# Layout of the streamed weights and the x loads, order of the first products, operands moved to PSUM, and places of four small chains in a two-layer trunk

## The chip, the cores and the metric

The kernel runs on one core of one Trainium2 chip. The metric is the device time of one execution, in microseconds (us), as the median of three runs. PE is the matrix engine (TensorE), DVE the vector engine, ACT the scalar engine, POOL the engine for general work (GpSimd), and SP the engine whose queue issues the weight loads. SBUF is the on-chip memory of all engines; PSUM holds what PE accumulates, and DVE and ACT can read and write it too.

## The reference

Two layers over a sequence of S = 256 positions with D = 1024 channels, in float32. Cut to what matters:

```python
for l in range(2):
    h = rmsnorm(x, norm_mix[l]); p = h @ w_in[l] + b_in[l]      # 6144 columns: xm, z, a, g, g1, g2
    y_m = mlstm_branch(p[xm], p[z], ...)                         # conv, q/k/v by blocks of 4, 4 heads, @ w_down
    y_c = silu(layernorm(dwconv31(p[a] * sigmoid(p[g])))) @ w_pw + b_pw
    x = x + (sigmoid(p[g1]) * y_m + sigmoid(p[g2]) * y_c) @ w_out[l]
    x = x + cross_attention(rmsnorm(x), rmsnorm(mem), wq, wk, wv, wo)
    x = x + conv_ffn(rmsnorm(x), w_up, dwconv3, w_down)          # 2816 hidden channels, gated
return rmsnorm(x, final_norm)
```

The mLSTM heads weigh their scores by exp(-max(m - u, mask)), a 256 x 256 matrix per head that is zero above the diagonal, and then multiply them with v.

## The kernel before

Activations lie with channels on the 128 partitions and the 256 positions along the row. A float32 operand is split into a high and a low part, and a product is the sum of three matmuls, high by high, high by low and low by high (`three`, lines 94 to 96), or of two instructions (`two`, lines 89 and 90) where a high part is multiplied with both parts of the other at once.

The weights are streamed. A chunk is 256 columns by 1024 rows, 1 MB; SP's queue loads it into one of three `raw` tiles (line 154, the first chunk in two loads of 128 columns, line 152). Each half of 128 columns is split into one of five `wsp` tiles: ACT casts the high part (line 173; line 171 in two pieces for the first half), and the low part, raw less high part, is taken by POOL (line 177, two instructions) or DVE (line 179, one) by the table `ON_POOL`, which lists for each kind of chunk the numbers of those that POOL takes. PE then makes 24 matmuls of 128x256 with each half. The chunks come in a fixed order: `xm` (0 to 3), `g` and `a`, `k`, `v`, `z`, `g1`, `g2`, `mdown`, `pw`, `out`, then attention (`q`, `wo`), then the network (`ug`, `uv`, `dn`). The tile framework reorders the instructions by priority within what the data allow; a helper that is told to act after a given product is called a hook, (j, k) being half j after product k.

The names that matter here:

- `u` is x times the norm's weights, split into parts (lines 262 and 263). The norm's factor is applied after the products, as a row: `stats` sums squares over channels by a matmul with a column of means (line 306), DVE adds epsilon (308), POOL takes the power -0.5 (310), and `to_row` turns the result into a row by a matmul with the identity (298). Layer 0 sums its squares on DVE first (lines 915, 916) into `ssum`; later `Stream.add` adds a square per channel block to `ssum` (341 or 339, then 342).
- `gate_weights` (lines 372 to 392) folds the gate's weights into the block-diagonal ones, and POOL builds block-diagonal tiles of them, `bb` (line 427). Line 491 is PE's first use.
- `head` (569 to 587): PE spreads a row of maxima over the partitions (`pm`, named `sm` in the trace), DVE makes the exponent (573, 575), ACT the exponential (577), and DVE multiplies by the scores `sc` (579; the tile `sc` is a part of `ws`), giving the weights `wt` of the head's matmuls (584, 587).
- Line 458 is the long row of taps of the 31-wide convolution, on DVE, with its sum `cv` in PSUM and its input `u` in SBUF.
- `swish` takes the row of the layer norm (310, 298) and applies it (711).

Of the kernel before, what the change touches and what calls it, by code (L numbers as in the profile page):

```python
# [15 lines left out]
P = 128  # L16
# [18 lines left out]
ON_POOL = {"xm": (2, 3), "g": (0, 1, 2, 3), "a": (0, 1, 2, 3), "k": (0, 1, 2, 3), "v": (0, 1),  # L35
           "z": (0, 2, 3), "g1": (0, 1, 2, 3), "g2": (0, 1), "wo": (0, 1, 2),
           "uv": tuple(range(11))}
# [16 lines left out]
def trunk(ctx, tc, xT, memT, pvec, wgr, w_in, ml_w_down, cv_w_pw, w_out, xa_wq, xa_wk, xa_wv, xa_wo,  # L54
# [53 lines left out]
    def cols(w, c0, k0=0, k1=KT):  # L108
        return w[c0 // 256, :, k0:k1, :]
# [35 lines left out]
    def emit_loads(upto):  # L145
        while st["dma"] < min(upto, len(chunks)):
# [3 lines left out]
            if i == 0:  # L150
                for sl in (slice(0, P), slice(P, 2 * P)):
                    nc.sync.dma_start(raws[i][:, :, sl], ap[:, :, sl])
            else:
                nc.sync.dma_start(raws[i], ap)
            st["dma"] += 1

    def emit_splits(upto):

        while st["split"] < min(upto, 2 * len(chunks)):
            i, j = divmod(st["split"], 2)  # L160
            emit_loads(i + 1)
            if chunks[i][0][0] == "v":
                r = raws[i][:, 2 * j:2 * j + 2, :]
            else:
                r = raws[i][:, :, j * P:(j + 1) * P]
            both = wsp.tile([P, 2] + list(r.shape[1:]), F32R, tag="wsp", name=nm("wsp"))
            hi, lo = both[:, 0], both[:, 1]
            if st["split"] == 0:
# [27 lines left out]
    with tc.high_priority():  # L196
        nc.scalar.dma_start(pvs[0][:, 0:KT], pvec[0][:, 0:KT])
        emit_loads(1)
        for c2 in range(4):
            loaded = nc.scalar.dma_start(xs[:, 2 * c2:2 * c2 + 2, :], xT[:, 2 * c2:2 * c2 + 2, :])  # L200
# [68 lines left out]

    def proj(key, x2, hooks=None, halves=False, bank=None):  # L270
# [3 lines left out]
        for j, w in weights(key):  # L274
            ps = (bank or acc)([P, 2, S] if halves else [P, S])
            if st["use"] == 1:

                for n, (a, b) in enumerate(((0, 0), (0, 1), (1, 0))):
                    for k in range(KT):
                        nc.tensor.matmul(ps, w[:, a, k, :], x2[:, k, b], start=(n + k == 0), stop=(n == 2 and k == KT - 1))  # L280
                yield j, ps
                continue
# [19 lines left out]
    def inv_rms(q, eps, free=True, rv=None):  # L302

        pt = pcv.tile([P, S], F32, tag="cv", name=nm("cm")) if free else sm([P, S])
        for t in range(2):
            nc.tensor.matmul(pt[:, t:t + 1], q[:, t * P:(t + 1) * P], mean1[:, 0:1], start=True, stop=True)
# [6 lines left out]
    class Stream:  # L313
# [17 lines left out]
        def add(self, c, ps):  # L331
# [4 lines left out]
            else:  # L336
                q = scr.tile([P, S], F32, tag="t2", name=nm("sq"))
                if c == KT - 1:
                    nc.vector.tensor_tensor(q, xs[:, c, :], xs[:, c, :], op=ALU.mult)
                else:  # L340
                    nc.scalar.activation(q, xs[:, c, :], AF.Square)
# [30 lines left out]
    def gate_weights(l):  # L372
# [17 lines left out]
        gs = sml.tile([P, 3, 8, 8], F32, tag="gs", bufs=1, name=nm("gs"))  # L390
        for w in range(3):
            nc.vector.tensor_reduce(gs[:, w], wg[:, w].rearrange("p c d g -> p c g d"), axis=AX.X, op=ALU.add)
        return pws, mq, gs

    def mix(l, x):
        gates = None if l else gate_weights(l)
        xc, hs = planes("xch")
        at, ready, norms = int(l == 0), [], list(range(4))
        hooks = {(0, 4): x.stats, (1, 1): x.to_row} if at else x.hooks()
        for i in range(4):  # L400
            for j, ps in proj(("xm", l, i), x.u, hooks if i == at else None,
                              bank=sm if i == 1 and at else None):
# [33 lines left out]
        pws, mq, gs = gates or gate_weights(l)  # L436
        build(mq, bqk)
        nc.vector.tensor_copy(bv[:, :, P:P + 8], gs[:, 2])
# [130 lines left out]
        def head(h):  # L569
            pm = sm([P, S])  # L570
            nc.tensor.matmul(pm, pick[:, h:h + 1].broadcast_to([36, P]), mrow, start=True, stop=True)
            wt = scr.tile([P, 384], F32, tag="t2", name=nm("wt"))
            nc.vector.scalar_tensor_tensor(wt[:, 0:256], pm, ucol[:, 0, h:h + 1], later,
                                           op0=ALU.subtract, op1=ALU.max)
            nc.vector.scalar_tensor_tensor(wt[:, 256:384], pm[:, P:S], ucol[:, 1, h:h + 1],
# [434 lines left out]
```

## Time and profile before

| | before |
|---|---|
| runs | 1103.79, 1099.6, 1101.84 us; median 1101.84 |
| profiled execution | 1103.6 us, of which the span from the first to the last instruction is 1101.9 |
| PE, PEld | busy 1075.8 us (98%), 1009.8 us (92%) |
| DVE, ACT, POOL | 857.4 us (78%), 694.1 us (63%), 438.6 us (40%) |
| mean granted clock of PE | 0.986 of full speed |
| DMA | 185.39 MB, 168 GB/s; the weights' queue 45.6% of 16 engines |

A row of a timeline is a start, a busy time, engine, line, operation, output<-inputs and a count, with the idle time of the engine ahead of it and what ended that in brackets. The clock is given as a share of full speed: 1.00 is the level of 2.4 GHz, about 0.51 that of 1.2 GHz.

### The profile page before, as it was taken

What the parts mean: (1) busy time and instruction counts of PE and PEld (TensorE: products, weight loads), DVE (VectorE), ACT (ScalarE), POOL (GpSimd) and SP (SyncE); (2) the same over time, 40 slices, a digit from 0 to 9 for tenths busy, and PEclk for the clock granted to TensorE, in tenths of its full rate; (3) what the DMA queues carried; (4) which work ended last, traced back from release to release, by engine and by line L of the source; (5) the groups of instructions that cost most, each with busy time, mean ns of one, the idle gap of its engine ahead of it and who ended that gap; (6) DMA issues with size and microseconds to landing.
All of it is one profiled execution on the core that took longest, in us unless ns stands there. A gap on an engine that the chain in (4) does not pass through costs nothing.

```text
span 1101.9 us, 19628 instructions
## 1 busy us (share of the span) xinstructions
PE 1075.8 (98%) x7642; PEld 1009.8 (92%) x7642; DVE 857.4 (78%) x1701; ACT 694.1 (63%) x1132; POOL 438.6 (40%) x351
## 2 busy tenths in 40 slices
PE   7999799999999999999999999999999999999996
PEld 7999689999999998888899998999999999888885
DVE  5788898978866887776668998998787578877753
ACT  5887365556555678774458766565545558877641
POOL 3858448610023445330048584782000434544000
PEclk8999899999999999999999999999999999999998
DMA  6535335445443445555545263545454244554541
GB/s 225 226 116 175 131 116 205 178 153 207 177 156 112 159 179 199 191 181 186 207 154 214 86 208 135 191 159 195 183 188 166 107 153 145 205 211 170 190 152 39
DMA packets 28957, 185.39 MB, mean 168 GB/s; under 512 B 3136, under 2 KB 5184, under 8 KB 7744
## 3 DMA queue, kind: packets, MB, share of 16 engines
q1 hardware_dynamic: 27280, 179.32, 45.6%
q10 hardware_dynamic: 1584, 4.82, 1.3%
q8 instruction: 60, 0.98, 0.4%
q14 instruction: 33, 0.27, 0.1%
HBM read 183.08 MB, written 1.05 MB: 167 GB/s over the span
## 4 chain that ended last, share of the span: by engine, by line
PE 92%; DVE 3%; ACT 1%; DMA 1%; POOL 1%; issue 1%; ACTq 0%; DVEq 0%
PE acc L89 20%; PE acc L95 18%; PE acc L94 18%; PE acc L96 18%; PE acc L90 10%; PE sm L94 2%; PE sm L95 1%; PE sm L96 1%; DVE wt L579 1%; ACT wsp L173 1%; PE sm L512 1%; DMA xs<-in_xT_dram 1%; DVE u L263 1%; PE sm L501 1%; PE sm L491 1%
## 5 line engine op out<-in xcount | busy, mean ns | idle before, releaser
L177 POOL TENSOR_TENSOR wsp<-raw,wsp 128x512 fp32r<-128x512 f32 x312 | 405.5, 1331 | 367.2 <-ACT wsp L173 361.7
L173 ACT CAST wsp<-raw 128x1024 fp32r<-128x1024 f32 (+1 forms) x343 | 353.6, 1036 | 193.0 <-PE acc L96 103.8
L179 DVE TENSOR_TENSOR wsp<-raw,wsp 128x1024 fp32r<-128x1024 f32 (+1 forms) x188 | 230.7, 1228 | 79.6 <-ACT wsp L173 77.4
L89 PE MATMUL acc<-x,wsp 128*128 128x512 f32 x576 | 203.6, 399 | 0.0
L458 DVE SCALAR_TENSOR_TENSOR cv<-u,pv,cv 128x256 f32<-128x256 f32 x464 | 193.4, 479 | 3.1 <-ACT cv L451 3.1
L94 PE MATMUL acc<-x,wsp 128*128 128x256 f32 x640 | 183.3, 287 | 0.0
L95 PE MATMUL acc<-x,wsp 128*128 128x256 f32 x640 | 181.6, 284 | 0.0
L96 PE MATMUL acc<-x,wsp 128*128 128x256 f32 x640 | 181.2, 283 | 0.0
L90 PE MATMUL acc<-x,wsp 128*128 128x256 f32 x576 | 161.8, 281 | 0.0
L89 PEld LDWEIGHTS acc<-x,wsp 128*128 128x128 f32 x576 | 108.2, 188 | 26.9
L89 PE MATMUL acc<-hh,wsp 128*128 128x512 f32 x352 | 124.5, 399 | 0.0
L95 PEld LDWEIGHTS acc<-x,wsp 128*128 128x128 f32 x640 | 122.7, 192 | 0.3
L94 PEld LDWEIGHTS acc<-x,wsp 128*128 128x128 f32 x640 | 122.6, 192 | 0.4 <-issue 0.2
L96 PEld LDWEIGHTS acc<-x,wsp 128*128 128x128 f32 x640 | 122.7, 192 | 0.2 <-issue 0.2
L90 PEld LDWEIGHTS acc<-x,wsp 128*128 128x128 f32 x576 | 108.8, 189 | 0.0
L310 POOL TENSOR_TENSOR rv<-rv,mhalf 128x2 f32<-128x2 f32 x9 | 7.2, 804 | 248.1 <-DVE rv L308 248.1
L95 PE MATMUL acc<-u,wsp 128*128 128x256 f32 x360 | 102.6, 286 | 0.7 <-DVE u L263 0.7
L94 PE MATMUL acc<-u,wsp 128*128 128x256 f32 x360 | 103.0, 289 | 0.0
L96 PE MATMUL acc<-u,wsp 128*128 128x256 f32 x360 | 102.5, 286 | 0.0
L855 DVE SCALAR_TENSOR_TENSOR fy<-u,pv,fy 128x256 f32<-128x256 f32 x176 | 84.1, 483 | 19.9 <-ACT fy L852 18.3
L90 PE MATMUL acc<-hh,wsp 128*128 128x256 f32 x352 | 98.9, 281 | 0.0
L89 PEld LDWEIGHTS acc<-hh,wsp 128*128 128x128 f32 x352 | 66.1, 188 | 16.4
(263 smaller groups left out, 2419.4 us busy)
## 6 DMA issues: line engine op xcount, KB each, us to landing
raw<-in_w_in_dram SPq DMA_DIRECT2D x47, 1024.0 KB, 4.8
raw<-in_ffn_w_up_dram SPq DMA_DIRECT2D x44, 1024.0 KB, 4.8
raw<-in_ffn_w_down_dram SPq DMA_DIRECT2D x16, 1024.0 KB, 4.8
raw<-in_xa_wk_dram SPq DMA_DIRECT2D x8, 1024.0 KB, 4.7
raw<-in_xa_wv_dram SPq DMA_DIRECT2D x8, 1024.0 KB, 5.1
raw<-in_ml_w_down_dram SPq DMA_DIRECT2D x8, 1024.0 KB, 4.7
raw<-in_cv_w_pw_dram SPq DMA_DIRECT2D x8, 1024.0 KB, 4.8
raw<-in_w_out_dram SPq DMA_DIRECT2D x8, 1024.0 KB, 4.7
```

The source lines that it names most:

```text
L89: nc.tensor.matmul(ps, a[:, 0], b, start=first, stop=False)
L90: return nc.tensor.matmul(ps[:, 1], a[:, 1], b[:, 0], start=False, stop=last)
L94: nc.tensor.matmul(ps, a[:, 0], b[:, 0], start=first, stop=False)
L95: nc.tensor.matmul(ps, a[:, 0], b[:, 1], start=False, stop=False)
L96: return nc.tensor.matmul(ps, a[:, 1], b[:, 0], start=False, stop=last)
L173: nc.scalar.copy(hi, r)
L177: nc.gpsimd.tensor_tensor(lo[:, sl], r[:, sl], hi[:, sl].bitcast(F32), op=ALU.subtract)
L179: nc.vector.tensor_tensor(lo, r, hi.bitcast(F32), op=ALU.subtract)
L263: nc.vector.scalar_tensor_tensor(lo, src, g, hi.bitcast(F32), op0=ALU.mult, op1=ALU.subtract)
L458: nc.vector.scalar_tensor_tensor(o, u31[:, c, k:k + S], col(l, "cdw", c * CK + k), cv[j], op0=ALU.mult, op1=ALU.add)
L491: nc.tensor.matmul(ps[:, j, :], bqk[:, c, :], xc[:, c, :], start=True, stop=True)
L855: nc.vector.scalar_tensor_tensor(y[:, j, :], u[:, j, k:k + S], col(l, "fdw", 3 * c + k), y[:, j, :], op0=ALU.mult, op1=ALU.add)
```

## The change

- The weights lie in DRAM by 128 columns instead of 256, so that a half of a chunk is a contiguous 4 KB on each partition; x comes in two loads instead of four.
- The first chunk's products are made by part over both halves (`proj_first`): the high weights of both halves first, then the low ones. The second half's cast is made in two pieces as well, and the splits of two further halves are issued ahead of the squares.
- The eight squares of layer 0 go to PE as they are, sixteen matmuls of one column each, instead of being added on DVE first. The hooks of statistics and row stand later in their chunks, in both layers.
- `Stream.add` keeps its squares in PSUM and makes all of them on ACT.
- The gate's weights of layer 0 are made after the `xm` chunks instead of ahead of them; one copy is gone.
- `head` keeps mask and exponential in PSUM.
- `swish` comes after the first `mdown` chunk instead of ahead of it.
- The low parts of `xm` chunk 2 and of `uv` chunk 0 pass from POOL to DVE, in both layers.

```diff
-ON_POOL = {"xm": (2, 3), "g": (0, 1, 2, 3), "a": (0, 1, 2, 3), "k": (0, 1, 2, 3), "v": (0, 1),
+ON_POOL = {"xm": (3,), "g": (0, 1, 2, 3), "a": (0, 1, 2, 3), "k": (0, 1, 2, 3), "v": (0, 1),
-           "uv": tuple(range(11))}
+           "uv": tuple(range(1, 11))}
...
     def cols(w, c0, k0=0, k1=KT):
-        return w[c0 // 256, :, k0:k1, :]
+        return w[c0 // P:c0 // P + 2, :, k0:k1, :].rearrange("j p k c -> p j k c")
...
             if i == 0:
-                for sl in (slice(0, P), slice(P, 2 * P)):
-                    nc.sync.dma_start(raws[i][:, :, sl], ap[:, :, sl])
+                for j in range(2):
+                    nc.sync.dma_start(raws[i][:, j], ap[:, j])
...
-                r = raws[i][:, :, j * P:(j + 1) * P]
+                r = raws[i][:, j]
...
-            if st["split"] == 0:
+            if st["split"] < 2:
...
-        for c2 in range(4):
-            loaded = nc.scalar.dma_start(xs[:, 2 * c2:2 * c2 + 2, :], xT[:, 2 * c2:2 * c2 + 2, :])
+        for sl in (slice(0, 4), slice(4, 8)):
+            loaded = nc.scalar.dma_start(xs[:, sl, :], xT[:, sl, :])
...
+    def proj_first(key, x2):
+
+        done = [(w, acc([P, S])) for _, w in weights(key)]
+        for j, a, b in ((0, 0, 0), (0, 0, 1), (1, 0, 0), (1, 0, 1), (0, 1, 0), (1, 1, 0)):
+            w, ps = done[j]
+            for k in range(KT):
+                nc.tensor.matmul(ps, w[:, a, k, :], x2[:, k, b], start=(a + b + k == 0), stop=(a == 1 and k == KT - 1),
+                                 skip_group_check=True)
+        return enumerate(ps for _, ps in done)
...
-    def inv_rms(q, eps, free=True, rv=None):
+    def inv_rms(pieces, eps, free=True, rv=None):
...
         for t in range(2):
-            nc.tensor.matmul(pt[:, t:t + 1], q[:, t * P:(t + 1) * P], mean1[:, 0:1], start=True, stop=True)
+            for n, q in enumerate(pieces):
+                nc.tensor.matmul(pt[:, t:t + 1], q[:, t * P:(t + 1) * P], mean1[:, 0:1],
+                                 start=(n == 0), stop=(n == len(pieces) - 1))
...
-                q = scr.tile([P, S], F32, tag="t2", name=nm("sq"))
-                if c == KT - 1:
-                    nc.vector.tensor_tensor(q, xs[:, c, :], xs[:, c, :], op=ALU.mult)
-                else:
-                    nc.scalar.activation(q, xs[:, c, :], AF.Square)
+                q = sm([P, S])
+                nc.scalar.activation(q, xs[:, c, :], AF.Square)
                 nc.vector.tensor_tensor(self.s, self.s, q, op=ALU.add)
             self.split(c)
...
         def hooks(self):
-            return {(0, 6): self.stats, (1, 5): self.to_row}
+            return {(0, 7): self.stats, (1, 6): self.to_row}
...
-        gs = sml.tile([P, 3, 8, 8], F32, tag="gs", bufs=1, name=nm("gs"))
+        gs = sml.tile([P, 2, 8, 8], F32, tag="gs", bufs=1, name=nm("gs"))
         for w in range(3):
-            nc.vector.tensor_reduce(gs[:, w], wg[:, w].rearrange("p c d g -> p c g d"), axis=AX.X, op=ALU.add)
+            nc.vector.tensor_reduce(gs[:, w] if w < 2 else bv[:, :, P:], wg[:, w].rearrange("p c d g -> p c g d"),
+                                    axis=AX.X, op=ALU.add)
...
-        gates = None if l else gate_weights(l)
-        hooks = {(0, 4): x.stats, (1, 1): x.to_row} if at else x.hooks()
+        hooks = {(0, 5): x.stats, (1, 4): x.to_row} if at else x.hooks()
         for i in range(4):
-            for j, ps in proj(("xm", l, i), x.u, hooks if i == at else None,
-                              bank=sm if i == 1 and at else None):
+            for j, ps in (proj_first(("xm", l, i), x.u) if l + i == 0 else
+                          proj(("xm", l, i), x.u, hooks if i == at else None, bank=sm if i == 1 and at else None)):
...
-        pws, mq, gs = gates or gate_weights(l)
+        pws, mq, gs = gate_weights(l, bv)
         build(mq, bqk)
-        nc.vector.tensor_copy(bv[:, :, P:P + 8], gs[:, 2])
...
-            pm = sm([P, S])
-            nc.tensor.matmul(pm, pick[:, h:h + 1].broadcast_to([36, P]), mrow, start=True, stop=True)
+            pm = sm([P, 384])
+            nc.tensor.matmul(pm[:, 0:S], pick[:, h:h + 1].broadcast_to([36, P]), mrow, start=True, stop=True)
+            nc.vector.scalar_tensor_tensor(pm[:, S:], pm[:, P:S], ucol[:, 1, h:h + 1], later[:, 0:P],
+                                           op0=ALU.subtract, op1=ALU.max)
+            nc.vector.scalar_tensor_tensor(pm[:, 0:S], pm[:, 0:S], ucol[:, 0, h:h + 1], later,
+                                           op0=ALU.subtract, op1=ALU.max)
+            nc.scalar.activation(pm, pm, AF.Exp, scale=-1.0)
             wt = scr.tile([P, 384], F32, tag="t2", name=nm("wt"))
-            nc.vector.scalar_tensor_tensor(wt[:, 0:256], pm, ucol[:, 0, h:h + 1], later,
-                                           op0=ALU.subtract, op1=ALU.max)
-            nc.vector.scalar_tensor_tensor(wt[:, 256:384], pm[:, P:S], ucol[:, 1, h:h + 1],
-                                           later[:, 0:P], op0=ALU.subtract, op1=ALU.max)
-            nc.scalar.activation(wt, wt, AF.Exp, scale=-1.0)
             for o, n, m in ((0, 256, 0), (256, 128, 264)):
-                nc.vector.scalar_tensor_tensor(wt[:, o:o + n], sc[:, h, m:m + n], 1.0 / 16.0, wt[:, o:o + n],
+                nc.vector.scalar_tensor_tensor(wt[:, o:o + n], sc[:, h, m:m + n], 1.0 / 16.0, pm[:, o:o + n],
                                                op0=ALU.mult, op1=ALU.mult)
...
-        swish()
         ym = s1
         for i in range(4):
             for j, ps in proj(("mdown", l, i), o2):
                 c = 2 * i + j
                 nc.vector.tensor_tensor(ym[:, c, :], ps, s1[:, c, :], op=ALU.mult)
+            if i == 0:
+                swish()
...
-    with tc.high_priority():
-        with tc.issue_after(table.ins):
-            for c in range(8):
-                if c == 4:
-                    emit_splits(1)
-                x.split(c)
-    emit_splits(2)
+    with tc.high_priority(), tc.issue_after(table.ins):
+        for c in range(8):
+            if c == 4:
+                emit_splits(1)
+            x.split(c)
+    emit_splits(4)
     sq = [t2(F32, "sq") for _ in range(4)]
     for c2 in range(4):
         nc.scalar.activation(sq[c2], xs[:, 2 * c2:2 * c2 + 2, :], AF.Square)
-    for c2 in range(1, 4):
-        nc.vector.tensor_tensor(sq[0], sq[0], sq[c2], op=ALU.add)
-    nc.vector.tensor_tensor(x.s, sq[0][:, 0, :], sq[0][:, 1, :], op=ALU.add)
+    x.squares = [q[:, j, :] for q in sq for j in range(2)]
...
-        host[n] = _tiles(inp[n], 512 if n == "xa_wv" else 256)
+        host[n] = _tiles(inp[n], 512 if n == "xa_wv" else 128)
```

On PE, the first instructions of the program after the clock warm-up (L211) were, before (`acc_206` and `acc_235` are the sums of the first chunk's halves, `wsp_158` and `wsp_170` their weights):

```order
L211 MATMUL sm_99<-mean_96 128x128 x13
L280 MATMUL acc_206<-u_149,wsp_158 128x256 x24
L94 MATMUL acc_235<-u_149,wsp_170 128x256
L95 MATMUL acc_235<-u_149,wsp_170 128x256
L96 MATMUL acc_235<-u_149,wsp_170 128x256
```

and are now (`acc_189` and `acc_193` are the two sums, `sm_247` that of the next chunk's first half):

```order
L211 MATMUL sm_97<-mean_94 128x128 x13
L276 MATMUL acc_189<-u_147,wsp_156 128x256 x22
L276 MATMUL acc_193<-u_147,wsp_168 128x256 x16
L276 MATMUL acc_189<-u_147,wsp_156 128x256 x2
L276 MATMUL acc_193<-u_147,wsp_168 128x256 x8
L94 MATMUL sm_247<-u_147,wsp_172 128x256
```

The 48 matmuls are the same; those of the second half now stand among those of the first, and its low weights come last.

On PE, in the second chunk's first half, the statistics of layer 0 stood, before, after 17 of its 24 matmuls:

```order
L95 MATMUL sm_266<-u_149,wsp_200 128x256
L96 MATMUL sm_266<-u_149,wsp_200 128x256
L306 MATMUL cm_282<-mean_96,ssum_148 128x1 x2
L94 MATMUL sm_266<-u_149,wsp_200 128x256
L95 MATMUL sm_266<-u_149,wsp_200 128x256
```

and stand now after 18 (`sq_178` to `sq_181` hold two channel blocks of squares each):

```order
L96 MATMUL sm_247<-u_147,wsp_172 128x256
L310 MATMUL cm_266<-mean_94,sq_178 128x1 x2
L310 MATMUL cm_266<-mean_94,sq_179 128x1 x2
L310 MATMUL cm_266<-mean_94,sq_180 128x1 x2
L310 MATMUL cm_266<-mean_94,sq_181 128x1 x2
L310 MATMUL cm_266<-mean_94,sq_178 128x1 x2
L310 MATMUL cm_266<-mean_94,sq_179 128x1 x2
L310 MATMUL cm_266<-mean_94,sq_180 128x1 x2
L310 MATMUL cm_266<-mean_94,sq_181 128x1 x2
L94 MATMUL sm_247<-u_147,wsp_172 128x256
```

Two matmuls became sixteen; each is two instructions in the trace (x2 here is x4 there).

On DVE, at the first head of layer 0 (`k` and `acc` are attention's keys, `cv` the convolution's sums), before:

```order
L257 TENSOR_TENSOR k_1276<-acc_1283,k_1276 128x256
L257 TENSOR_TENSOR k_1276<-acc_1312,k_1276 128x256
L573 SCALAR_TENSOR_TENSOR wt_1366<-sm_1364,ucol_1274,later 128x256
L575 SCALAR_TENSOR_TENSOR wt_1366<-sm_1364,ucol_1274,later 128x128
L458 SCALAR_TENSOR_TENSOR cv_1232<-u_133,pv_86,cv_1232 128x256
L608 TENSOR_TENSOR acc_1416<-acc_1416,mem_row 128x256
L579 SCALAR_TENSOR_TENSOR wt_1366<-ws_185,wt_1366 128x256
L579 SCALAR_TENSOR_TENSOR wt_1366<-ws_185,wt_1366 128x128
```

and now:

```order
L257 TENSOR_TENSOR k_1282<-acc_1318,k_1282 128x256
L574 SCALAR_TENSOR_TENSOR sm_1370<-sm_1370,ucol_1280,later 128x128
L460 SCALAR_TENSOR_TENSOR cv_1238<-u_131,pv_86,cv_1238 128x256
L576 SCALAR_TENSOR_TENSOR sm_1370<-sm_1370,ucol_1280,later 128x256
L610 TENSOR_TENSOR acc_1422<-acc_1422,mem_row 128x256
L460 SCALAR_TENSOR_TENSOR cv_1237<-u_131,pv_86,cv_1237 128x256
L460 SCALAR_TENSOR_TENSOR cv_1238<-u_131,pv_86,cv_1238 128x256
L581 SCALAR_TENSOR_TENSOR wt_1375<-ws_533,sm_1370 128x256
L581 SCALAR_TENSOR_TENSOR wt_1375<-ws_533,sm_1370 128x128
```

The product with the scores (579, now 581) reads one tile in SBUF and one in PSUM where it read two in SBUF, and two taps of the convolution stand ahead of it that stood elsewhere; on PE 43 matmuls lie between the row of maxima and the head's first product, where 35 lay.

## Rows read from the trace of the kernel before

**Rows 1.** The page, busy time of each engine, its share of the span and instructions.
```profile
PE 1075.8 (98%) x7642; PEld 1009.8 (92%) x7642; DVE 857.4 (78%) x1701; ACT 694.1 (63%) x1132; POOL 438.6 (40%) x351
```
**Rows 2.** What PE waited for: us in total, times, longest us.
```profile
PE sm L584 <- DVE wt L579: 5.6, 3, 4.6
...
PE acc L280 <- ACT wsp L171: 3.4, 1, 3.4
...
PE sm L96 <- DVE wsp L179: 0.6, 1, 0.6
```
**Rows 3.** Stretches: length, busy times (instructions), clock, DMA share, GB/s.
```profile
10.46:17.40 6.94, 6.94 (x30) 6.60 (x31) 6.18 (x11) 5.93 (x13) 0.00 (x0) 0.51 1.02 411
...
27.64:31.05 3.41, 3.41 (x19) 3.41 (x18) 1.57 (x4) 2.57 (x6) 3.41 (x4) 0.51 0.92 377
33.00:50.42 17.42, 17.42 (x145) 17.34 (x145) 14.39 (x35) 14.82 (x26) 16.52 (x12) 1.00 0.55 204
...
117.42:123.20 5.78, 5.76 (x18) 4.54 (x19) 3.35 (x11) 0.87 (x4) 0.00 (x0) 0.51 0.55 181
...
365.00:380.00 15.00, 14.45 (x119) 14.03 (x118) 12.25 (x19) 8.25 (x15) 7.83 (x7) 1.00 0.51 188
...
563.50:566.90 3.40, 3.40 (x18) 3.40 (x18) 0.00 (x0) 1.04 (x1) 2.19 (x3) 0.51 0.00 0
...
895.00:910.00 15.00, 14.45 (x119) 14.03 (x118) 11.47 (x20) 7.57 (x11) 6.22 (x5) 1.00 0.45 147
```
**Rows 4.** Timeline of the opening, all engines.
```profile
6.85 0.91 ACT L262 ACTIVATE u<-xs,pv 128x256 fp32r<-128x256 f32 x2 [1.36 <-DMA xs<-in_xT_dram]
...
9.00 0.91 ACT L262 ACTIVATE u<-xs,pv 128x256 fp32r<-128x256 f32 x2 [1.25 <-DMA xs<-in_xT_dram]
...
9.81 1.12 ACT L171 CAST wsp<-raw 128x512 fp32r<-128x512 f32 x2
...
10.46 6.12 PE L280 MATMUL acc<-u,wsp 128*128 128x256 f32 x24 [3.44 <-ACT wsp L171]
...
21.70 0.50 PE L306 MATMUL cm<-mean,ssum 128*128 128x1 f32 x4
...
22.06 0.36 PE L94 MATMUL sm<-u,wsp 128*128 128x256 f32 x1
```
**Rows 5.** DMA from 0 to 40 us, GB/s in 40 slices of 1 us.
```profile
GB/s 0 3 118 170 153 236 342 383 395 429 439 418 459 401 401 408 406 365 393 164 16 0 0 0 0 0 0 164 401 401 442 410 352 188 434 352 8 0 16 0
```
**Rows 6.** Timeline of PE: the row of layer 0's first norm.
```profile
26.82 0.71 PE L298 MATMUL sm<-ident,rv 128*128 128x128 f32 x4 [1.06 <-POOL rv L310]
```
**Rows 7.** Timeline of DVE, then of POOL, at layer 0's first head.
```profile
102.01 4.40 DVE L458 SCALAR_TENSOR_TENSOR cv<-u,pv,cv 128x256 f32<-128x256 f32 x11
...
111.86 5.63 DVE L579 SCALAR_TENSOR_TENSOR wt<-ws,wt 128x256 f32<-128x256 f32 x2
...
98.29 18.73 POOL L177 TENSOR_TENSOR wsp<-raw,wsp 128x512 fp32r<-128x512 f32 x15
```
**Rows 8.** Timeline of POOL, then of PE, around the gate's tiles of layer 0.
```profile
40.76 1.95 POOL L427 TENSOR_TENSOR bb<-mq,blk 128x1024 f32<-128x1024 f32 x1
...
50.26 1.02 PE L491 MATMUL sm<-xch,bb 128*128 128x256 f32 x4
```
**Rows 9.** Timeline of PE at the layer norm's row, layer 1.
```profile
771.13 0.71 PE L298 MATMUL sm<-ident,rv 128*128 128x128 f32 x4 [0.46 <-POOL rv L310]
```
**Rows 10.** Timeline of DVE, then PE, from layer 0's network into layer 1.
```profile
560.05 1.01 DVE L339 TENSOR_TENSOR sq<-xs 128x256 f32<-128x256 f32 x1
561.09 1.37 DVE L342 TENSOR_TENSOR ssum<-ssum,sq 128x256 f32<-128x256 f32 x1
...
562.52 0.61 PE L306 MATMUL cm<-mean,ssum 128*128 128x1 f32 x4 [1.29 <-DVE ssum L342]
```
**Rows 11.** Timeline of DVE: two low parts of the opening.
```profile
18.14 1.22 DVE L179 TENSOR_TENSOR wsp<-raw,wsp 128x1024 fp32r<-128x1024 f32 x1 [0.44 <-ACT wsp L173]
...
22.86 2.10 DVE L179 TENSOR_TENSOR wsp<-raw,wsp 128x1024 fp32r<-128x1024 f32 x1
```

More of the change, by code (lines that the diff above doesn't have):

```diff
@@ L275, in proj @@
             ps = (bank or acc)([P, 2, S] if halves else [P, S])
[L276 to L282, printed above, removed]
             for k in range(KT):
@@ L319, in __init__ @@
             self.s = sml.tile([P, S], F32, tag="ssum", bufs=1, name=nm("ssum"))
+            self.squares = [self.s]
             if gname != "nfin":
@@ L345, in hooks @@
         def hooks(self):
-            return {(0, 6): self.stats, (1, 5): self.to_row}
+            return {(0, 7): self.stats, (1, 6): self.to_row}
         def stats(self):
             with tc.high_priority(offset=300):
-                self.rv = inv_rms(self.s, 1e-6)
+                self.rv = inv_rms(self.squares, 1e-6)
         def to_row(self):
@@ L369, in normed, with gate_weights @@
             split_act(xn, self.n[:, sl])
-    def gate_weights(l):
+    def gate_weights(l, bv):
         o = _COLS["bd"]
@@ L692, in ln_stats @@
             nc.vector.tensor_tensor(qs[:, 0, :], qs[:, 0, :], qs[:, 1, :], op=ALU.add)
-            ln["rv"] = inv_rms(qs[:, 0, :], 1e-5)
+            ln["rv"] = inv_rms([qs[:, 0, :]], 1e-5)
         portions += [ln_mean] + [lambda c2=c2: ln_square(c2) for c2 in range(4)] + [ln_stats]
@@ L766, in mem_stats @@
     def mem_stats(sq):
-        inv_rms(sq[:, 0, :], 1e-6, False, mem_col)
+        inv_rms([sq[:, 0, :]], 1e-6, False, mem_col)
     def mem_rows():
@@ L936, in _chan, with _tiles @@
     return np.ascontiguousarray(a.T.reshape(KT, P, S).swapaxes(0, 1))
-def _tiles(w, c=256):
+def _tiles(w, c):
     import numpy as np
```

## The prediction

> **What bounds the kernel now.** The page gives PE 1075.8 of 1101.9 us [rows 1]: PE is the bound nearly everywhere, so the change can gain only where PE idles (26.1 us in all) or runs at the lower clock, and can lose only where it makes PE idle or gives it more work. The second view is PE's list of waits, which names the causes: 5.6 us for the heads' weights `wt`, of which one wait is 4.6; 3.4 for the first cast; 0.6 for one low part of DVE [rows 2]. The third is the table of stretches. Between 33.00 and 50.42 PE has no gap at clock 1.00, 145 matmuls in 17.42 us: one each 0.12 us, a half of a chunk (24) 2.88. Four stretches stand at 0.51: 10.46 to 17.40, 27.64 to 31.05, 117.42 to 123.20 and 563.50 to 566.90 [rows 3]. Each follows an idle of PE: 3.44, 1.06, 4.6 and 1.29 us [rows 2, 4, 6, 10]. So an idle is paid twice, by itself and by about half of the stretch behind it: 1.7, 2.9 and 1.7 us for the last three. Last, the timeline at these places shows what was late.
>
> **The opening.** PE starts at 10.46, when ACT has cast a quarter of the first half's weights; ACT waited for x at 6.85 and again at 9.00 [rows 4]. Now the first half of x must land once. In the DMA view the slices to 7 us hold 1.02 MB and those to 9 us 1.80 [rows 5]. Half of x and half of the first chunk are 1.0 MB, so at before's own rate they are there at 7.0; x alone (0.5 MB) would be at 5.7; the pessimistic bound is 9.00, when half of x was there before. I take 6.5, since the slices from 2 to 6 us are slow (118 to 236 GB/s) beside 400 later and the change makes those transfers longer: nearer to 5.7 and 7.0 than to 9.0. Then four high parts of u (0.455 each) and half a cast (0.56) [rows 4] give PE's start at 8.9. How fast it then goes: from the first product to the last of this chunk it took 21.70 less 17 matmuls of 0.12, that is 19.66, less 10.46: 9.2 us for 48, most of it at clock 0.51 [rows 3, 4]. The new order asks for both halves' high weights first and no DVE low weights until two thirds are done, so I keep the 9.2: it ends at 18.1 (bounds 17.1, if the lower clock ends sooner, and 20.6, from 9.00). From there to the second half of `xm` chunk 2: 72 matmuls, 8.64; the statistics; the row, 0.5 [rows 6]. The statistics: two matmuls, four instructions, moved the next product from 21.70 to 22.06, 0.36 us or 0.09 each [rows 4]; sixteen are 32 instructions, 2.9 us, all on PE, which pays for the DVE adds taken away. So 18.1 + 8.64 + 2.9 + 0.5 = 30.1. Before, counted alike from 22.06: 55 matmuls, 6.6, the row 0.5, the waits of 0.6 for DVE's low part and of 1.06 for the row [rows 2, 6], and the 1.7 of lower clock behind them: 32.5. Those two waits should go: the low part took 2.10 beside POOL, 1.22 alone [rows 11], and POOL now has no split until chunk 3; 21 matmuls still stand between statistics and row, 2.5 us, and POOL is free to take the power at once. **+2.4** (bounds -1.8, with the late x and the lower clock again, and +3.4).
>
> **The head.** In layer 0 line 579 takes 5.63 us for two instructions while POOL runs fifteen low parts back to back, 98.29 to 117.02, and ends 0.5 after they stop; line 458 runs eleven times at 0.40 through the same stretch [rows 7]. The two differ in their inputs: 579 reads two tiles in SBUF, 458 one in SBUF and one in PSUM. The moved operand makes 581 of the second kind, so I price it at 0.40 and 0.3, and the waits of 5.6 and the 2.9 of lower clock go: 8.5. The chain then is mask 0.8, exponential 0.5, the DVE rows queued between 2.0, product 0.7: 4.0 us against 43 matmuls, 5.2. I take **+8.2** (0 to 8.5). The Trainium skill, "SBUF — State Buffer", section "Who interferes with whom", says that a DVE instruction with two SBUF inputs and a GpSimd instruction that reads SBUF exclude each other for a whole instruction, and that one with at most one SBUF input doesn't contend. The trace agrees (5.63 against 0.40). The same rule speaks against the other edit, low parts on DVE: raw and high part both lie in SBUF; see the last rival.
>
> **Network into layer 1, and attention into the network.** At 562.52 PE waited 1.29 for a DVE add of 1.37 behind a square of 1.01 [rows 10]; the square goes to ACT, the add reads PSUM, and the statistics come after 39 matmuls instead of 24, 1.8 us later. The 1.29 and the 1.7 behind it go. What is late next is the row: 6 matmuls instead of 18 stand before it, 0.7 us, and the chain of epsilon and power was 1.1: a wait of 0.4. **+2.6** (0 to 3.0). From `wo` to `ug` PE idles 0.55 in each layer (14.45 of 15.00) [rows 3], while POOL takes `uv` chunk 0's low parts beside DVE's adds; with the adds reading PSUM and those low parts on DVE it should close: **+1.0** (0 to 1.1). DVE's two more splits of 1.22 there lie beside PE.
>
> **Gate, layer norm, tail.** The gate's second tile on POOL ended at 42.7; PE asks for it at 50.26 [rows 8]. It now stands seven splits behind the first row's power instead of four. Three splits are 7.5 (two instructions of 1.25 each, 18.73 over 15 [rows 7]), and that power comes some 2.4 earlier: it ends at 47.8 (sooner by whatever POOL waited for casts), and PE asks at 50.26 - 2.4 = 47.9, later still by a wait. **-0.3** (0 to -2.5, one split more). Line 298 of layer 1's layer norm waited 0.46 [rows 9] with 4 matmuls between statistics and row, and now has 44; layer 0's has 5 instead of 6, 0.1 lost: **+0.4** (-0.1 to 0.5). At the end the last square goes from DVE to ACT: **-0.1** (0 to -0.3).
>
> **At nothing.** Rows of 4 KB for the weights: the weights' queue is far from full where PE never waits (DMA share 0.55 between 33 and 50 [rows 3]); if they cost a tenth, the loads would still land ahead. Two more low parts a chunk on DVE cost 2.4 us of DVE beside 5.76 of PE; the cover is DVE's idle time, and without it the last rival's price holds.
>
> **Sum.** 2.4 + 8.2 + 2.6 + 1.0 - 0.3 + 0.4 - 0.1 = 14.2. The profiled execution took 1103.6 (span 1101.9 and 1.7 around it): 1089.4. It stands 1.8 above the median of the runs, so I forecast **1087.6** for the median.
>
> **Rivals.**
>
> *The opening gives nothing.* The halves of x land together with the weights, ACT's chain starts at 9.0, and PE pays the 2.9 of statistics. For it: x comes in larger pieces, and no row shows one. Against it: the two waits and the 1.7 behind them don't hang on x. 1087.6 + 2.4 = 1090.0; at its bound of -1.8, 1091.8.
>
> *The head still waits.* The change doesn't do what it says: POOL's run ends where it ended, and something else of the chain (the two taps ahead of 581, the exponential in PSUM, behind a cast of 1.05 on ACT) is late by as much. For it: several rows now stand between mask and product. Against it: 458 at 0.40 in the same run of POOL. 1087.6 + 8.2 = 1095.8, and within 0.5% of before with any small loss elsewhere.
>
> *Slower: low parts held up behind POOL.* The eight low parts moved to DVE (two halves of `xm` chunk 2 and two of `uv` chunk 0, in each layer) read two tiles in SBUF, as 579 did. Where one falls into a run of POOL without gaps it takes about 5.4 instead of 1.22, PE waits 4.2, and 2.9 of lower clock follow: 7.1 each; in layer 0 the second one of chunk 2 also stands ahead of the four DVE instructions that free PE's first sums. Two such stalls leave 1101.8, no change; from the third on the kernel is slower, 1108.9. By the skill's section above this would be the usual case wherever POOL runs; 2.10 beside four instructions of POOL [rows 11] is the milder form that this kernel shows for a low part. Against three: POOL's own splits move away from just these places, and around the moved ones it waits for casts.
>
> **Chances and range.** Forecast 0.63 (own range 1085 to 1090.5), opening nothing 0.18, head still waiting 0.10, low parts held up 0.09 (half with one or two stalls, 1094.7 or 1101.8; half with three or more). What this kernel's measurement can tell from no change is about 0.5%, 5.5 us: faster is below 1096.3. Faster holds the first two, half of the third and a little of the last, and I set 0.86; same 0.09; slower 0.05. The range runs from 1084.0 to 1095.8, the head's case. Every term at its upper bound is 16.5, or 1085.3; the rest below is for idle of the 26.1 that no term names. Above lie about 0.12, below 0.05.
>
> **What would show it.** PE's first product at 8.4 to 9.5; 32 instructions of statistics at some 0.09; no wait for `wt` above 0.5 and no clock of 0.5 around 118 or 564; line 581 at 0.3 to 0.45 within POOL's run; a row wait of about 0.4 into layer 1; no idle from `wo` to `ug`. The prediction is wrong if x lands after 8.5, if sixteen matmuls of one column take much more than 2.9, or if a low part of 179 takes 3 us or more with PE waiting for it.

## The result and the profile after

The changed kernel takes 1088.61 us (median of 4 runs, 1088.43 to 1090.76) beside 1102.82 (4 runs): a ratio of 0.988, 95% interval 0.9855 to 0.9906. Three of the four runs lie between 1088.43 and 1088.64 (mean clock 0.993), one at 1090.76 (0.991). The profiled execution took 1088.43 with a span of 1086.7, which is 15.2 less than before; 14.2 were forecast. The page's line of busy times and PE's list of waits, whole, are now:

```profile
PE 1070.4 (99%) x7670; PEld 1008.0 (93%) x7670; DVE 844.1 (78%) x1697; ACT 696.6 (64%) x1141; POOL 414.8 (38%) x335
```

```profile
PE acc L276 <- ACT wsp L171: 4.0, 1, 4.0
PE sm L301 <- POOL rv L315: 2.5, 3, 1.3
PE cm L310 <- DVE ssum L345: 1.8, 1, 1.8
PE sm L211 <- DVE zero L212: 1.1, 1, 1.1
```

The waits for `wt` and for DVE's low part [rows 2] are gone; the start (4.0), the end of the program (1.8 and 1.0) and layer 0's layer norm's row (1.3) are the larger ones left. To see where the time came from, the table pairs the same instruction in both traces.

| place (instruction before, after) | before | after | gained so far |
|---|---|---|---|
| memory's norm, row to column form (298, 301) | 106.08 | 106.41 | -0.3 |
| fourth head's first product (584, 586) | 138.10 | 129.57 | 8.5 |
| after the heads, first transpose (663, 665) | 170.24 | 160.44 | 9.8 |
| attention, layer 0 (806, 809) | 329.27 | 319.56 | 9.7 |
| inside the network, layer 0 (pairs on DVE and ACT, 460 to 500, median) | | | 10.6 |
| layer 1, ahead of its layer norm (680, 682) | 759.61 | 746.62 | 13.0 |
| attention, layer 1 (806, 809) | 861.30 | 847.77 | 13.5 |
| last norm (298, 301) | 1093.79 | 1079.28 | 14.5 |
| end of the span | 1101.9 | 1086.7 | 15.2 |

Two thirds come at the heads, and the opening gave nothing. The timeline of the opening (engines apart: two rows of ACT, four of PE) answers to [rows 4, 6]:

```profile
8.11 1.71 ACT L262 ACTIVATE u<-xs,pv 128x256 fp32r<-128x256 f32 x4 [4.41 <-DMA xs<-in_xT_dram]
9.72 1.12 ACT L171 CAST wsp<-raw 128x512 fp32r<-128x512 f32 x2
...
10.38 8.79 PE L276 MATMUL acc<-u,wsp 128*128 128x256 f32 x48 [3.97 <-ACT wsp L171]
...
21.17 3.63 PE L310 MATMUL cm<-mean,sq 128*128 128x1 f32 x32
24.65 0.36 PE L94 MATMUL sm<-u,wsp 128*128 128x256 f32 x1
...
28.15 1.05 PE L301 MATMUL sm<-ident,rv 128*128 128x128 f32 x4
```

x's first half comes at 8.11, PE starts at 10.38 as it did at 10.46, and the statistics hold it from 21.17 to 24.65. In the table of stretches (columns as in [rows 3]) the second one is at half clock again, although PE had no gap in it, nor ahead of it since its first product; the other four stretches have no gap and no half clock:

```profile
21.17:24.65 3.48, 3.48 (x34) 3.48 (x33) 0.00 (x0) 0.00 (x0) 0.00 (x0) 1.00 0.20 77
26.07:29.48 3.41, 3.41 (x19) 3.41 (x18) 0.05 (x1) 0.86 (x2) 3.41 (x4) 0.50 0.68 199
...
112.00:126.00 14.00, 14.00 (x96) 12.38 (x94) 11.51 (x37) 7.97 (x20) 10.70 (x10) 1.00 0.57 187
365.00:380.00 15.00, 15.00 (x127) 15.00 (x126) 13.23 (x29) 13.91 (x23) 5.11 (x4) 1.00 0.42 141
...
893.00:908.00 15.00, 15.00 (x128) 15.00 (x127) 13.22 (x29) 13.70 (x23) 5.10 (x4) 1.00 0.42 141
```

At the first head (DVE, then POOL), the answer to [rows 7]:

```profile
113.39 0.62 DVE L581 SCALAR_TENSOR_TENSOR wt<-ws,sm 128x256 f32<-128x256 f32 x2 [0.33 <-ACT sm L578]
...
98.30 18.79 POOL L177 TENSOR_TENSOR wsp<-raw,wsp 128x512 fp32r<-128x512 f32 x15
```

POOL's run is what it was, and the product inside it takes 0.62 instead of 5.63.

### The profile page after: what moved, and what is told of

The parts are those of the page before. It is cut to its first block, busy times and chain, and to the rows that moved or that the text cites. A ratio compares the mean times of both kernels' runs of the same rounds, so it can differ in the third digit from the quotient of the medians.

```text
span 1086.7 us, 19678 instructions
## 1 busy us (share of the span) xinstructions
PE 1070.4 (99%) x7670; PEld 1008.0 (93%) x7670; DVE 844.1 (78%) x1697; ACT 696.6 (64%) x1141; POOL 414.8 (38%) x335
## 5 line engine op out<-in xcount | busy, mean ns | idle before, releaser
L177 POOL TENSOR_TENSOR wsp<-raw,wsp 128x512 fp32r<-128x512 f32 x296 | 380.6, 1316 | 241.5 <-ACT wsp L173 212.2
L179 DVE TENSOR_TENSOR wsp<-raw,wsp 128x1024 fp32r<-128x1024 f32 (+1 forms) x196 | 242.6, 1240 | 81.1 <-ACT wsp L173 79.0
L96 PE MATMUL acc<-u,wsp 128*128 128x256 f32 x352 | 99.9, 284 | 0.0
L95 PE MATMUL acc<-u,wsp 128*128 128x256 f32 x352 | 99.7, 284 | 0.0
L94 PE MATMUL acc<-u,wsp 128*128 128x256 f32 x352 | 99.7, 285 | 0.0
```

Source lines behind the costliest of these rows:

```text
L94: nc.tensor.matmul(ps, a[:, 0], b[:, 0], start=first, stop=False)
L95: nc.tensor.matmul(ps, a[:, 0], b[:, 1], start=False, stop=False)
L96: return nc.tensor.matmul(ps, a[:, 1], b[:, 0], start=False, stop=last)
L177: nc.gpsimd.tensor_tensor(lo[:, sl], r[:, sl], hi[:, sl].bitcast(F32), op=ALU.subtract)
L179: nc.vector.tensor_tensor(lo, r, hi.bitcast(F32), op=ALU.subtract)
```

## The experiments

Each run's time is its median; that of before on the same chips was 1101.88 to 1101.91. All but e2 are edits of the changed kernel.

**e1, the exponential back in SBUF.**

```diff
-            nc.scalar.activation(pm, pm, AF.Exp, scale=-1.0)
             wt = scr.tile([P, 384], F32, tag="t2", name=nm("wt"))
+            nc.scalar.activation(wt, pm, AF.Exp, scale=-1.0)
...
-                nc.vector.scalar_tensor_tensor(wt[:, o:o + n], sc[:, h, m:m + n], 1.0 / 16.0, pm[:, o:o + n],
+                nc.vector.scalar_tensor_tensor(wt[:, o:o + n], sc[:, h, m:m + n], 1.0 / 16.0, wt[:, o:o + n],
```

> The changed kernel with one operand moved back: mask still in PSUM, but the exponential is written to the SBUF tile wt, so that the product with the scores (line 581) reads two SBUF tiles; the order of all instructions stays. Theory (the operand decides: two SBUF inputs wait for the end of POOL's run): line 581 takes some 5 us once in layer 0, PE waits 3 to 4.6 us for it and has a stretch at half clock behind it: 1088.6 + 6 to 10 = 1094.5 to 1098.5. Rival (the order decides: two more rows of DVE and 43 instead of 35 matmuls ahead of the head's product gave the time): line 581 stays under 1 us, 1088.6 within 1.

1095.99 us, ratio 0.9952 (0.9937 to 0.9968), 7.4 more than the changed kernel. Timeline of DVE and of POOL, the stretch behind, and PE's wait:

```profile
115.65 4.12 DVE L581 SCALAR_TENSOR_TENSOR wt<-ws,wt 128x256 f32<-128x256 f32 x2 [0.34 <-ACT wt L579]
...
100.56 18.72 POOL L177 TENSOR_TENSOR wsp<-raw,wsp 128x512 fp32r<-128x512 f32 x15
...
119.53:122.95 3.42, 3.24 (x7) 2.13 (x7) 2.17 (x8) 0.43 (x2) 0.00 (x0) 0.50 0.78 237
...
PE sm L586 <- DVE wt L581: 4.3, 3, 3.4
```

Up to the product the order of instructions is that of the changed kernel; it starts at 115.65 and ends 0.5 after POOL's run (119.28). The operand decides, not the order: the rival fell. Behind the product the scheduler moves some instructions of the heads and of the stages around them, so the 7.4 us hold a little of that as well.

**e2, the new head alone** on the kernel before.

> The kernel before with the new head alone (mask and exponential in PSUM, nothing else). Theory (the head is worth two thirds of the change): no wait for wt, no half clock at 117, 1102.8 - 8 to 10 = 1093 to 1095. Rival (the gain at the head needed the other edits too, POOL's run reaching it earlier): under 5 us, 1098 or more.

1092.75, ratio 0.9917 (0.99 to 0.9933): 9.1 us of 14. The head needs no other edit. Paired as in the table, the trace of e2 gains 8.9 from memory's norm (105.92 beside 106.08) to the fourth head's first product (129.07 beside 138.10), and 10.1 to the first transpose (159.95 beside 170.24).

The trace shows one thing more. Into layer 1, where this run has no edit, PE waits as long as before [rows 10], but the clock behind the wait is 1.00 and not 0.51. The third line is of the kernel before, behind its wait of 1.26 for layer 0's layer norm:

```profile
PE cm L306 <- DVE ssum L342: 1.3, 1, 1.3
...
552.11:560.00 7.89, 7.89 (x66) 7.89 (x67) 4.45 (x12) 5.21 (x10) 5.79 (x5) 1.00 0.24 69
...
243.52:251.00 7.48, 7.48 (x62) 7.48 (x63) 6.11 (x10) 6.29 (x10) 0.00 (x0) 1.00 0.31 103
```

So a wait of 1.3 us is not always followed by a half-clock stretch, and the 1.7 us behind it at 562.52 [rows 3, 10] need not be there in every execution.

**e3, layer 0's squares added on DVE** as before.

```diff
-    x.squares = [q[:, j, :] for q in sq for j in range(2)]
+    for c2 in range(1, 4):
+        nc.vector.tensor_tensor(sq[0], sq[0], sq[c2], op=ALU.add)
+    nc.vector.tensor_tensor(x.s, sq[0][:, 0, :], sq[0][:, 1, :], op=ALU.add)
```

> The changed kernel with the squares of layer 0 added on DVE again: two statistics matmuls instead of sixteen. Theory (the sixteen matmuls of one column cost 3.5 us of PE, and the half clock at 26.1 to 29.5 follows them, since PE had no idle before it): 3.1 us less of PE and no second half-clock stretch, 1088.6 - 3.1 - 1.7 = 1083.8, as far as DVE's 2.5 us of adds are hidden. Rival 1 (the half clock comes in any case some 9 us after the first stretch): 1085.5. Rival 2 (PE waits for DVE's adds or for the low parts queued behind them): 1087 to 1089.

1093.59, ratio 0.9922 (0.9907 to 0.9937): 5 slower than the changed kernel, against every theory. The table of stretches and PE's waits:

```profile
22.00:30.00 8.00, 7.40 (x63) 7.20 (x62) 2.01 (x6) 4.03 (x7) 8.00 (x7) 1.00 0.53 160
145.91:148.75 2.84, 0.00 (x1) 0.00 (x1) 2.84 (x6) 2.33 (x5) 0.45 (x1) 1.00 0.00 0
149.74:153.15 3.41, 3.41 (x9) 2.64 (x8) 3.29 (x7) 2.65 (x5) 1.67 (x2) 0.50 0.87 309
```

```profile
PE sm L95 <- DVE wsp L179: 2.8, 1, 2.8
```

The opening did what the theory said: no half clock from 22 to 30, and 2.1 us gained where memory's norm stands (104.29 beside 106.41). But the scheduler places everything behind it anew, and at 145.91 PE waits 2.8 for a low part of DVE, with a half-clock stretch behind; by the next layer norm the gain has become a loss of 5.6 (line 301 at 240.22 beside 234.59), and from there on it is 5.0. The low part came late because DVE came to it late; it took no longer than elsewhere:

```profile
143.91 1.25 DVE L629 TENSOR_TENSOR va<-va,rr 128x8 f32<-128x8 f32 x1 [1.53 <-POOL va L628]
...
147.48 1.21 DVE L179 TENSOR_TENSOR wsp<-raw,wsp 128x1024 fp32r<-128x1024 f32 x1
```

This run can't price the statistics alone; e5 keeps the order.

**e4, the old table `ON_POOL`.**

> The changed kernel with the old table: low parts of xm chunk 2 and uv chunk 0 on POOL again. Theory (with the squares in PSUM the adds no longer collide with POOL, but low parts of DVE with POOL would; the moved low parts give about half of the 0.9 us from wo to ug and nothing in the opening): 1088.6 + 0 to 1.5. Rival (the moved low parts carry the gains from wo to ug and into layer 1, 0.9 + 2.1 + 0.9): 1092 to 1093. Second rival (the low parts on DVE cost time): under 1088.

1089.07, ratio 0.9887 (0.9864 to 0.9911): 0.5 of loss. In the traces the loss is 0.2 all through layer 0 and 0.9 at the end, the size that the theory gave; the collision of DVE's adds with POOL doesn't come back, and from `wo` to `ug` PE loses nothing. What is left of it is one wait of 0.7 for a part of `u` into layer 1.

**e5, single-pass statistics.**

```diff
-    sq = [t2(F32, "sq") for _ in range(4)]
+    sq = [t2(F32R, "sq") for _ in range(4)]
...
+        m = 2 if len(pieces) > 1 else 1
...
-                nc.tensor.matmul(pt[:, t:t + 1], q[:, t * P:(t + 1) * P], mean1[:, 0:1],
+                nc.tensor.matmul(pt[:, m * t:m * t + m], q[:, t * P:(t + 1) * P],
+                                 (mean_r if m > 1 else mean1)[:, 0:m],
```

> The changed kernel with layer 0's squares and the column of means as rounded single-pass operands (F32R): still sixteen statistics matmuls at the same place (two columns each instead of one, the second unused), one instruction each instead of two; every other instruction keeps its place but for one small DVE copy ahead of the warm-up. The mean of squares is a little less exact. Theory (PE pays for the statistics by the instruction, and the half clock at 26.1 follows the 3.5 us of one-column matmuls): 1.7 us less of PE, and the half-clock stretch, another 1.7, goes or stays: 1088.6 - 1.7 = 1086.9, or 1085.2. Rival (PE would wait for the squares or the row instead): 1088.6.

1085.73, ratio 0.985 (0.9825 to 0.9875), 2.9 less than the changed kernel. PE's timeline, and a stretch of the table:

```profile
22.08 1.84 PE L313 MATMUL cm<-mean_r,sq 128*128 128x2 f32 x16
23.78 0.36 PE L94 MATMUL sm<-u,wsp 128*128 128x256 f32 x1
...
26.00:30.00 4.00, 4.00 (x36) 4.00 (x35) 2.53 (x7) 2.49 (x6) 4.00 (x4) 1.00 0.76 262
```

The statistics take 1.70 (22.08 to 23.78) instead of 3.48, and the half clock behind them is gone, with nothing else moved. Number of instructions, columns and operand type change together here, so which of them the clock follows is not shown.

**e6, x in four loads; e7, weights in DRAM by 256 columns.** Neither moves an instruction of the engines.

```diff
-        for sl in (slice(0, 4), slice(4, 8)):
+        for sl in (slice(0, 2), slice(2, 4), slice(4, 6), slice(6, 8)):
             loaded = nc.scalar.dma_start(xs[:, sl, :], xT[:, sl, :])
```

```diff
-        return w[c0 // P:c0 // P + 2, :, k0:k1, :].rearrange("j p k c -> p j k c")
+        return w[c0 // 256, :, k0:k1, :]
...
-                for j in range(2):
-                    nc.sync.dma_start(raws[i][:, j], ap[:, j])
+                for sl in (slice(0, P), slice(P, 2 * P)):
+                    nc.sync.dma_start(raws[i][:, :, sl], ap[:, :, sl])
...
```

> The changed kernel with x loaded in four pieces of two channel blocks again; nothing else moves. Theory (the halves landed at 8.1 instead of the 6.5 that was forecast because x now shares the time with the first chunk's weights; four pieces let ACT start at 6.9 but end with the last piece): PE's first product between 9.6 and 10.4, 1088.6 - 0 to 0.8. Rival (fewer, larger pieces are what keeps the first product from coming later): 1088.6 + 0.5 to 1.5.

> The changed kernel with the weights in DRAM by 256 columns again (8 KB on each partition, the first chunk's halves in pieces of 512 bytes), the order of all instructions as in the changed kernel. Theory (the layout matters for the first chunk alone; the weights' queue has room): within 1 us of 1088.6. Rival (contiguous halves make casts and low parts or loads cheaper all along): 1090 or more. Second rival (the shorter rows cost DMA time, 47741 packets instead of 28957): 1087 or less.

e6: 1092.95, ratio 0.9907 (0.9878 to 0.9936); e7: 1087.35, ratio 0.986 (0.9827 to 0.9893). Rows of ACT (first uses of x) and PE, and a stretch, of e6:

```profile
7.63 0.91 ACT L262 ACTIVATE u<-xs,pv 128x256 fp32r<-128x256 f32 x2 [2.63 <-DMA xs<-in_xT_dram]
9.70 0.91 ACT L262 ACTIVATE u<-xs,pv 128x256 fp32r<-128x256 f32 x2 [1.16 <-DMA xs<-in_xT_dram]
...
13.63 0.51 ACT L262 ACTIVATE u<-xs,pv 128x256 fp32r<-128x256 f32 x1 [1.15 <-DMA xs<-in_xT_dram]
...
14.19 7.55 PE L276 MATMUL acc<-u,wsp 128*128 128x256 f32 x42 [1.08 <-ACT u L262]
...
25.94:32.77 6.83, 6.83 (x33) 6.83 (x34) 1.29 (x2) 1.04 (x1) 3.94 (x3) 0.50 0.23 71
```

and of e7:

```profile
7.25 1.70 ACT L262 ACTIVATE u<-xs,pv 128x256 fp32r<-128x256 f32 x4 [3.51 <-DMA xs<-in_xT_dram]
...
9.51 9.19 PE L276 MATMUL acc<-u,wsp 128*128 128x256 f32 x48 [3.29 <-ACT wsp L171]
```

My theory on e6 fell: the first product comes at 11.17, the last piece of x at 13.6, PE stalls a second time, and the loss is 4.3. Not all of this is the loads' doing. In the traces 2.6 is lost by the start of the statistics (23.74 beside 21.17), and 1.6 more behind it, where the half clock lasts 6.83 instead of 3.41 us; e1 and e9 show the same with x in two loads (last section). The rival held, larger than it said. Half of x was there at 9.00 (its rows 2 KB, those of the weights on the other queue 512 bytes [rows 4]), 7.25 (4 KB beside 512 bytes, e7), 8.11 (4 KB beside 4 KB), 9.70 (2 KB beside 4 KB, e6). So beside either layout x comes earlier in longer rows, which here also means fewer loads, and beside shorter rows of the weights. The new layout alone costs 0.9 us at the first product (10.38 beside 9.51) and gives nothing later that shows: e7's span is 0.4 below that of the changed kernel, its median 1.3, and all of its times lie below those of the changed kernel. The theory held within its bound by the span, and just missed it by the median.

**e8, the squares of `Stream.add` as before; e9, these and the old table; e10, the old hooks as well.**

```diff
-                q = sm([P, S])
-                nc.scalar.activation(q, xs[:, c, :], AF.Square)
+                q = scr.tile([P, S], F32, tag="t2", name=nm("sq"))
+                if c == KT - 1:
+                    nc.vector.tensor_tensor(q, xs[:, c, :], xs[:, c, :], op=ALU.mult)
+                else:
+                    nc.scalar.activation(q, xs[:, c, :], AF.Square)
```

> The changed kernel with Stream.add as before: squares in SBUF, the last one on DVE. Theory (squares in PSUM, and off DVE, give the 2.1 us into layer 1 and most of the 0.9 us from wo to ug in each layer): 1088.6 + 2 to 4. Rival (those came from the moved low parts and the later hooks): 1088.6 + 0 to 0.5.

> The changed kernel with both the squares of Stream.add (SBUF, last one on DVE) and the table of low parts as before; the later hooks stay. Undone one at a time they cost 0.2 and 0.5 us. Theory (either edit alone removes most of the collision of DVE's adds with POOL's low parts, so that only both together bring it back): 1088.6 + 2 to 4, with an idle of PE into layer 1 and from wo to ug. Rival (the later hooks hide the collision by themselves): 1088.6 + 0 to 1.

> The same with the hooks of statistics and row of all later norms at their old places as well. Theory of the run ahead of it (the two edits share the gain, the hooks add little): within 1 us of that run. Rival (the hooks carry it): that run stays near 1088.6, this one shows the waits of the kernel before, 1.3 us and its half clock into layer 1, 0.55 from wo to ug in each layer: 1088.6 + 3 to 5.

e8: 1088.81, ratio 0.9876 (0.9848 to 0.9904), no loss: the theory fell. e9: 1094.74, ratio 0.9933 (0.9912 to 0.9955). e10: 1092.2, ratio 0.9914 (0.9894 to 0.9934). PE's waits, one row of e9 and one of e10; then an add of DVE in a run of POOL's low parts in e9, with that run, and the add at the same place in e4:

```profile
PE acc L95 <- DVE u L263: 3.7, 3, 1.3
```

```profile
PE cm L310 <- DVE ssum L348: 3.6, 4, 1.9
```

```profile
357.75 1.30 DVE L348 TENSOR_TENSOR ssum<-ssum,sq 128x256 f32<-128x256 f32 x1 [0.98 <-ACT sq L347]
...
357.47 5.61 POOL L177 TENSOR_TENSOR wsp<-raw,wsp 128x512 fp32r<-128x512 f32 x4 [10.78 <-ACT wsp L173]
...
355.52 0.42 DVE L345 TENSOR_TENSOR ssum<-ssum,sm 128x256 f32<-128x256 f32 x1 [0.96 <-ACT sm L344]
```

In e9's trace 2.4 of its loss lie in the opening, which the edit doesn't touch (mostly a longer half clock, last section), and 4.2 where both edits act, behind attention in layer 0. Each undone alone cost 0.2 or 0.5. Each by itself parts DVE's two-SBUF adds from POOL's low parts; only with both gone do they meet again. With the add reading PSUM (e4) it takes 0.42 inside POOL's run, with two operands in SBUF (e9) 1.30; in e8 POOL has no low part there. The hooks only shift which wait PE sees, for `u` (e9) or for `ssum` (e10): without the 2.4 of the opening e9 would stand at 1092.3, where e10 is, and e10's trace loses 3.3 over the same stretch, so the hooks gave nothing that these runs show.

**e11, single-pass statistics and 256 columns; e12, the same with 20 matmuls of warm-up instead of 13** (`WARM = 20`).

> The changed kernel with single-pass statistics of layer 0 (as in the run above) and the weights in DRAM by 256 columns. Theory (the two gains are at different stretches of the opening, 2.9 and 1.2): 1084.5 within 0.8. Rival (both shorten the way to the same next wait, x's second half): 1085.7.

> The same with 20 instead of 13 matmuls of warm-up ahead of the first product, which fill PE's idle time up to about 9.3 us; nothing else moves. Theory (the half clock of 6.8 us at the first chunk follows PE's idle of 3.3 to 4 us ahead of it): no half clock there, the 48 products in 6 to 7 us instead of 9.2, as far as ACT and DVE supply them: 2 to 3 us less than the run ahead of it, 1081.5 to 1082.5. Rival (the half clock comes whatever PE does before, or the first chunk is bound by ACT's and DVE's splits): no change.

e11: 1084.61, ratio 0.9843 (0.9825 to 0.9862). The gains add up: 4.0 less than the changed kernel, 1.1 less than e5. e12: 1084.08, ratio 0.9834 (0.9815 to 0.9853), 0.5 less, within the spread of its own runs (1082.8 to 1085.0). A stretch of e12, and PE's rows:

```profile
12.30:15.71 3.41, 3.41 (x18) 3.41 (x18) 2.89 (x4) 3.41 (x6) 0.00 (x0) 0.50 1.09 398
...
9.14 0.74 PE L278 MATMUL acc<-u,wsp 128*128 128x256 f32 x4 [1.24 <-ACT wsp L171]
10.46 7.87 PE L278 MATMUL acc<-u,wsp 128*128 128x256 f32 x44 [0.58 <-ACT u L264]
```

In e12's profile the half clock at the first chunk is 3.41 instead of 6.83 us; in e8's, with the old warm-up and 5.1 us of idle time ahead of PE's start, it is 3.41 as well, so the warm-up is not shown to have done it:

```profile
11.10:14.52 3.42, 3.42 (x14) 2.90 (x14) 3.00 (x6) 3.42 (x9) 0.00 (x0) 0.50 0.98 387
```

Most of what it frees is lost again: PE waits 0.58 for `u`, and the next chunk's first product comes 0.6 earlier (18.17 beside 18.77). The outcome is near to the rival's, a first chunk that x and ACT bound.

No run undoes by itself the new order of the first chunk, the gate's later place or that of `swish`; what they gave is read from the traces alone.

## Why the prediction was right, and the step that failed

The forecast was 1087.6 and the time 1088.61, but that the two are so close is in part luck. The opening with the gate fell 2.4 short; the head gave 1.9 more than its term, the way from `wo` to `ug` 0.8 more, and the end 0.9 more, of which 0.7 has nothing to do with the change.

- **The head** was forecast at 8.2; the table has 8.8 up to the fourth head (-0.3 to 8.5), and e2 alone gave 9.1. The mechanism is shown by e1: the same order up to the product, the same run of POOL, 4.12 beside 0.62. Another 1.3 up to the first transpose (8.5 to 9.8) stood in no term. It too is the head's: e2 has 8.9 and 10.1 at the same two places.
- **From `wo` to `ug`**, forecast 1.0 for both layers, was 0.9 in each (9.7 to 10.6, 13.5 to 14.4). I had taken PE's idle time from its busy time, 0.55. A matmul's modelled end lies 0.28 after its start, while the next one may start after 0.12, so each gap reads up to 0.16 short. Counted it is right: 119 instructions in 15 us before [rows 3], 127 and 128 after; eight times 0.12 is 0.96. The cause was only half right: I put it down to two edits together, and e4 and e8 show that either of them is enough.
- **Into layer 1**, forecast 2.6, measured 2.4 (10.6 to 13.0). The wait of 1.29 is gone, and the row's wait that was to come, 0.4, is 0.21 (line 301 at 553.70). The other 1.7 was the half clock behind before's wait. I had put this down to the wait, "an idle is paid twice"; e2 and e10 have the wait (1.27) without it, so this part belongs to before's profiled execution as much as to the change. The forecast also takes off the 1.8 by which that execution stood above its median; whether it thus counts the same time twice, no run shows.
- **The opening**, forecast +2.4, and the gate, -0.3, gave -0.3 together. This is the step that failed, in three of its parts. x's first half came at 8.1, not 6.5: I reckoned with before's transfer rate and not with how x's and the weights' loads share the time; e7 shows that 0.9 of the 1.6 is the new layout, and the rest stays open. (The early bound of 5.7 is misread, too: at before's rate half a MB is there at 5.3.) The statistics took 3.48, not 2.9. And the half clock that was to go with the two waits stayed without any wait: the tie of half clock to idle time fails in this direction as well. e5 shows that it hangs on the long row of statistics, since it goes when that row is halved and nothing else is moved.
- **The layer norm** gave -0.1 and +0.5 as forecast. **The end** gave 0.1 instead of -0.1; the stores behind the last norm took 0.7 less (7.4 instead of 8.1 us), which no edit touches.

Of the rivals, "the opening gives nothing" came true with 1088.61 where it said 1090.0. The head did not wait. Low parts held up behind POOL did not come: the waits of the changed kernel hold no line 179. e3 shows what one late low part costs, a stall of 2.8 and a half-clock stretch, but not by that mechanism: it took its usual 1.21 and was late because DVE had waited for POOL's line 628 and for small instructions ahead of it.

The Trainium skill, "SBUF — State Buffer", section "Who interferes with whom", counts a DVE instruction with at most one SBUF input, outside its 2-port performance modes, as free of GpSimd. The measured 0.62 for two instructions in POOL's run, and 4.12 once one operand went back, agree.

## What to carry to other kernels

Where a vector instruction takes many times its usual time beside another engine, look at where its operands lie before you look at the order; here one operand moved back to SBUF cost 7.4 us (e1), and the head in PSUM gave 9.1 of 14 (e2). Count instructions in a stretch instead of trusting busy time to show idle time. And an edit that fixes its own place can move the scheduler's order elsewhere and lose more there (e3): price a step by a variant that leaves the order alone, as e5 did.

## What the hardware showed that I had not expected

A half-clock stretch can come without any gap. In the changed kernel PE worked without a pause from 10.38; its 32 statistics instructions of one column each took 3.48 us, and 1.4 us behind them, at 26.07, the clock fell to 0.50 for 3.41 us. With 16 single-pass instructions of two columns, 1.70 us (e5), it didn't fall. And waits of 1.3 us came with a half-clock stretch in one execution and without in others (e2).

The length of that stretch also differs between executions of one order: 3.41 in the changed kernel's profile, 6.83 in that of e1, whose opening runs the same instructions and where the clock falls within the row of statistics (from 21.84 on):

```profile
23.96:30.79 6.83, 6.83 (x34) 6.83 (x34) 1.29 (x2) 1.05 (x1) 3.80 (x3) 0.50 0.22 61
```

This is worth 1.6 us, from the first statistics instruction to memory's norm (86.8 in e1, 85.2 in the changed kernel); e6 and e9 have the same 6.83. The openings of e1 and e9 lie 2.3 and 2.4 behind in all, since their statistics already start 0.7 later. The profiles of e3, e5, e11 and e12, with short statistics and no wait above 0.6 behind them, have no second stretch in the opening.
